# Scan decays formed from running sums that a DMA spreads over the partitions

## The chip, the cores and the metric

One core of a Trainium2 chip runs the whole program. The metric is device time in microseconds, as the median of several runs. The engines are named as in the profile: PE is TensorE (PEld its weight loads), DVE is VectorE, ACT is ScalarE, POOL is GpSimd, SP is the engine that issues most DMAs.

## What is computed

The reference is a backbone of two layers over 256 latent tokens with 256 context tokens ahead of them. Layer 0 is attention beside a convolution module, then a dense feed-forward. Layer 1 is a bidirectional state-space mixer (a chunked scan), then a feed-forward with two of eight experts for each token. The change is in the scan. For one direction the reference has, with chunks of 128 tokens:

```python
a = (dt * a_coef).reshape(b, nc, CHUNK, SSM_GROUPS, HEADS_PER_GROUP)
a_cs = jnp.cumsum(jnp.moveaxis(a, 2, -1), axis=-1)
...
lower = jnp.tril(jnp.ones((CHUNK, CHUNK), dtype=bool))
seg = jnp.exp(jnp.where(lower, a_cs[..., :, None] - a_cs[..., None, :], -jnp.inf))
cb = jnp.einsum('bclgn,bcsgn->bcgls', cc, bc)
y_diag = jnp.einsum('bcgls,bcgels,bcsgep->bclgep', cb, seg, xc)
y_off = jnp.einsum('bclgn,bcgepn,bcgel->bclgep', cc, start, jnp.exp(a_cs))
```

The second direction is the same on the flipped sequence, and both results are added, with a skip term `d_skip * x`. There are 32 heads in 4 groups of 8. `a_coef` is negative, so all running sums fall.

## The kernel before

The program is written as units (a projection of 512 output columns, say), which a `run` loop walks through; generators such as the convolution and the scan run beside them, a few steps after each unit (`later`, `tick`). A scheduler then sets the order on each engine from this program order, from priorities and from a simulated timeline. Each engine runs its own list strictly in that order.

The stage around the change is layer 1's mixer, 745 to 1055 us. TensorE projects the hidden state in units `odd_b`, `odd_c`, four `odd_x` and four `odd_z`; each weight is split into a high part (ACT, L161 or, for the output projection, L157) and a low part (DVE or POOL in turn, L164; DVE, L158), and each product is three matmuls (L243 to L245). ACT copies the sums of a projection into padded tiles (L1050); a convolution of seven taps follows, one tap on ACT (L1066) and six on DVE (L1072), then a Silu (L1126) and transposes (L1088). The output projection `odd_out` ends the stage, and the expert layer follows, whose weights stream through the buffers that the stage leaves.

The scan (`odd_ssd`) is called once for each of the four groups, as soon as its convolution is done. It forms the states at the block borders (L1178 to L1196), then works on two latent blocks of 128 tokens, and in each on two units of four heads; that makes 16 units. In a unit, with partitions as source tokens s and columns as target tokens l:

- ACT (L1215) and POOL (L1217) multiply triangular masks with the high and the low part of the decay exponents, into two pairs of tiles `tri`; four matmuls (L1232, with the strict masks GTr and LTr as weights) add them up to the segment sums of both directions in one PSUM tile `pD`; ACT takes exp (L1235) into `E`.
- DVE masks the products of C and B once per block (L1205, L1206: `cb`); POOL multiplies them with the step sizes of each direction (L1225: two tiles `cd`), DVE adds the two (L1228) and multiplies with E (L1236).
- Four matmuls (L1240) multiply E with x. Per block, two matmuls add the part of the states (L1243), POOL forms the skip term (L1245), DVE adds up (L1248 to L1252), and the gate follows (L1257, L1258).

`odd_dt_fin` forms the step sizes `dt` (one column each per head and direction: 0 to 31 forward, 32 to 63 backward) and the exponents once, ahead of the scan; TensorE forms their running sums there (L986, L987) into `pcv`, from which exp gives `ecum`. Tiles come from rings of buffers: `tri` has 4, `cd` 3, `E` 2, the PSUM tag `t` 3.

## Time and profile before

| what | value |
|---|---|
| median of 3 runs | 1942.05 us (1939.05 to 1944.78) |
| profiled execution | 1943.61 us |
| its span | 1941.8 us |
| mean granted TensorE clock | 0.962 of full |
| busy: PE, DVE, ACT, POOL | 1796.3, 728.4, 509.5, 259.1 us |
| HBM read | 486.07 MB |

The profile gives busy times of each engine, a picture of the span in 40 slices (48.5 us each), the chain of work that ended last, and groups of equal instructions. A busy share over the whole span is a mean over stages that have different limits; so the stage of the scan is read by itself, in windows. Matmuls are pipelined: one of 512 columns is shown with 390 ns, while equal ones start closer together.

### The profile page before, as it was taken

The numbers are of one execution on the slowest core, as the hardware profiler recorded it, in microseconds if no ns is written. First come the engines' busy times: TensorE is split into PE (matmuls) and PEld (weight loads), VectorE is DVE, ScalarE is ACT, GpSimd is POOL, SyncE is SP. The second block draws the span as 40 slices with busy tenths as digits, with TensorE's granted clock in tenths as the row PEclk, the third lists the DMA queues.
The fourth block names the chain that finished last, engine by engine and source line by source line (L and its number), as shares of the span: only waits on it lengthen the run. The fifth ranks groups of instructions, "written<-read, shape, count | busy, mean of one in ns | idle before, by whom it ended". The sixth has DMA issues, their size and how long they took to land.

```text
span 1941.8 us, 33657 instructions
## 1 busy us (share of the span) xinstructions
PE 1796.3 (93%) x14444; PEld 1120.8 (58%) x14444; DVE 728.4 (38%) x1118; ACT 509.5 (26%) x927; POOL 259.1 (13%) x231
## 2 busy tenths in 40 slices
PE   6999998999999989988888899999998999899964
PEld 3775356788888868766666445445534464436411
DVE  3396545334343457889987210101010101001001
ACT  3434453321222246655564200100000000001000
POOL 0064000000000024465663000000000000000000
PEclk8999989999999999999999899999999999999975
DMA  7443665323223233212145899999999999999995
GB/s 290 170 162 137 235 188 182 130 87 109 87 87 109 87 122 109 87 64 89 65 162 195 304 386 418 412 418 416 418 417 418 417 416 409 418 418 413 418 412 205
DMA packets 126538, 489.47 MB, mean 252 GB/s; under 512 B 10752, under 2 KB 17704, under 8 KB 97704
## 3 DMA queue, kind: packets, MB, share of 16 engines
q1 hardware_dynamic: 126376, 487.18, 65.2%
q8 instruction: 117, 1.92, 0.4%
q14 instruction: 45, 0.37, 0.1%
HBM read 486.07 MB, written 1.08 MB: 251 GB/s over the span
## 4 chain that ended last, share of the span: by engine, by line
PE 64%; DMA 19%; DVE 11%; ACT 3%; issue 2%; POOL 1%; SPq 0%; DVEq 0%; ACTq 0%; POOLq 0%
PE h L1515 17%; PE g L243 9%; PE g L244 9%; DMA t<-in_od_ex_w_dram 9%; PE g L245 9%; DMA raw<-in_od_ex_w_dram 8%; PE y L1580 7%; DVE cv L1072 6%; PE g L347 1%; PE h L1468 1%; PE o L775 1%; PE g L752 1%; DVE whl L164 1%; DMA raw<-in_ev_w_in_dram 1%; PE h L1604 1%
## 5 line engine op out<-in xcount | busy, mean ns | idle before, releaser
L1515 PE MATMUL h<-t,xe 128*32 128x512 f32 (+1 forms) x2576 | 252.7, 542 | 12.8 <-DMA t<-in_od_ex_w_dram 12.7
L1515 PE MATMUL h<-raw,xe 128*32 128x384 f32 (+1 forms) x2288 | 230.2, 551 | 13.6 <-DMA raw<-in_od_ex_w_dram 13.6
L244 PE MATMUL g<-t,whl 128*128 128x512 f32 (+1 forms) x608 | 238.0, 392 | 0.0
L245 PE MATMUL g<-t,whl 128*128 128x512 f32 (+1 forms) x608 | 235.9, 393 | 0.8 <-POOL whl L164 0.8
L243 PE MATMUL g<-t,whl 128*128 128x512 f32 (+1 forms) x608 | 233.9, 396 | 0.7 <-ACT t L1161 0.7
L164 DVE TENSOR_TENSOR whl<-raw,whl 128x1024 fp32r<-128x1024 f32 x109 | 138.6, 1274 | 199.2 <-ACT whl L161 198.7
L161 ACT CAST whl<-raw 128x1024 fp32r<-128x1024 f32 x129 | 134.8, 1051 | 262.7 <-PE g L245 230.4
L1515 PEld LDWEIGHTS h<-t,xe 128*32 128x32 f32 x2576 | 92.2, 110 | 164.6 <-issue 109.0
L1526 DVE TENSOR_TENSOR g<-g,h 128x512 f32<-128x512 f32 (+1 forms) x38 | 23.6, 621 | 432.7 <-issue 273.4
L428 POOL TENSOR_SCALAR rsv<-sst 128x1 f32<-128x1 f32 (+1 forms) x15 | 5.2, 346 | 1303.3 <-DVE sst L421 1303.2
L244 PE MATMUL g<-whl,t 128*128 128x512 f32 (+1 forms) x432 | 169.7, 395 | 4.9 <-DVE whl L164 3.4
L1515 PEld LDWEIGHTS h<-raw,xe 128*32 128x32 f32 x2288 | 82.4, 111 | 153.1 <-issue 95.8
L245 PE MATMUL g<-whl,t 128*128 128x512 f32 (+1 forms) x432 | 165.6, 391 | 0.0
L243 PE MATMUL g<-whl,t 128*128 128x512 f32 (+1 forms) x432 | 162.3, 395 | 2.5 <-DVE t L641 1.2
L1580 PE MATMUL y<-t,hT 128*32 128x256 f32 x2336 | 136.9, 391 | 13.1 <-DMA t<-in_od_ex_w_dram 13.1
L1523 ACT ACTIVATE g<-h 128x512 f32<-128x512 f32 (+1 forms) x38 | 20.7, 544 | 451.0 <-PE h L1515 451.0
L243 PEld LDWEIGHTS g<-t,whl 128*128 128x128 f32 x608 | 116.4, 192 | 28.7 <-issue 2.6
L245 PEld LDWEIGHTS g<-t,whl 128*128 128x128 f32 x608 | 116.0, 191 | 25.2 <-issue 1.9
L244 PEld LDWEIGHTS g<-t,whl 128*128 128x128 f32 x608 | 116.7, 192 | 23.6 <-issue 1.0
L1580 PE MATMUL y<-raw,hT 128*32 128x256 f32 x1920 | 111.1, 387 | 8.9 <-DMA raw<-in_od_ex_w_dram 8.9
L1580 PEld LDWEIGHTS y<-t,hT 128*32 128x32 f32 x2336 | 74.4, 112 | 73.8 <-DMA t<-in_od_ex_w_dram 21.1
L1594 DVE TENSOR_TENSOR ys<-y,g2r 128x512 f32<-128x512 f32 (+1 forms) x12 | 6.6, 577 | 262.5 <-PE y L1580 262.5
(348 smaller groups left out, 2232.0 us busy)
## 6 DMA issues: line engine op xcount, KB each, us to landing
t<-in_od_ex_w_dram SPq DMA_DIRECT2D x130, 1024.0 KB, 19.5
raw<-in_od_ex_w_dram SPq DMA_DIRECT2D x110, 1024.0 KB, 19.8
t<-in_od_ex_w_dram SPq DMA_DIRECT2D x68, 768.0 KB, 15.0
raw<-in_od_ex_w_dram SPq DMA_DIRECT2D x60, 768.0 KB, 14.9
raw<-in_ev_ff_w_dram SPq DMA_DIRECT2D x32, 1024.0 KB, 5.4
raw<-in_ev_ada_w_dram SPq DMA_DIRECT2D x24, 1024.0 KB, 6.9
raw<-in_od_ada_w_dram SPq DMA_DIRECT2D x24, 1024.0 KB, 5.3
raw<-in_od_w_in_dram SPq DMA_DIRECT2D x20, 1024.0 KB, 5.1
```

What stands on the lines that cost most here:

```text
L161: self.nc.scalar.copy(hv, v[:, k0:k0 + m])
L164: eng.tensor_tensor(lv, v[:, k0:k0 + m], hv.bitcast(F32), op=ALU.subtract)
L243: mm(out, l[0], r[0], start=start, stop=False)
L244: mm(out, l[0], r[1], start=False, stop=False)
L245: mm(out, l[1], r[0], start=False, stop=stop)
L347: nc.tensor.matmul(st["p"][32 * j:32 * j + 32], self.cs[:, k, 6 - 2 * i:38 - 2 * i], wv, start=k < 4, stop=k >= 4, tile_position=(0, 32 * j))
L752: nc.tensor.matmul(sc[c][:, :nk], self.qT[s, r, b * P:(b + 1) * P], self.kT[s, :nk], start=True, stop=True, tile_position=(64 * c, 0))
L1072: nc.vector.scalar_tensor_tensor(v, pads[i + j][:, 0:ns, t:t + 256], self.cvw(t, c0 + i + j), v, op0=ALU.mult, op1=ALU.add)
L1515: nc.tensor.matmul(st[i][g][32 * p:32 * p + 32, :n], st["x"][:, k, 32 * g:32 * g + 32], wv[:, n * p:n * p + n], start=k == 0, stop=k == KD ...
L1523: nc.scalar.activation(st["g"][g], st[0][g][:, :n], AF.Silu)
L1526: nc.vector.tensor_mul(st["g"][g], st["g"][g], st[1][g][:, :n])
L1580: nc.tensor.matmul(st["y"][g // 2][32 * q:32 * q + 32, g % 2 * 256:g % 2 * 256 + 256], st["hT", s][:, c, g, 32 * p:32 * p + 32], wv[:, 256 ...
```

## The change

The segment sums are no longer added up by matmuls. Running sums of both directions are kept per token and head (`cum`: columns 0 to 31 the forward sum, 32 to 63 the backward sum less the forward one), transposed, written to DRAM once, and read back so that each partition holds a row of sums over the target tokens l: two DMAs per unit on ACT's queue, `f` with the forward sums and `r` with the difference, issued up to two units ahead (`load_rows`). ACT turns `r` into relu(column - row), DVE subtracts it from `f`, and ACT takes exp with the negated column `ncf` as its bias. For l after s the relu is 0 and the forward decay is left; for l ahead of s it turns it into the backward one. The step sizes come by one affine operation on ACT per head, `LE * (dt forward - dt backward) + dt backward`. The product of C and B is read from PSUM, unmasked. On the diagonal both directions count, so the backward share of it goes into the skip factor `skip`. The four `tri` buffers now hold the rows.

Per unit there were 8 ACT products, 2 + 2 POOL products, 4 matmuls, 1 exp of 128x512, 1 DVE sum and 1 DVE product; now there are 2 DMAs, 4 relus, 4 affine operations and 4 exps of 128x128 on ACT, and 1 DVE subtraction and 2 DVE products.

```diff
@@ -922,10 +922,6 @@
                     nc.sync.dma_start(dp[:, i, 32 * j:32 * j + 32], A[f"{nme}_{d}"].partition_broadcast(P)[:, 0])
             self.dsk = self.op.tile([P, 32], F32, name="dsk")
             nc.sync.dma_start(self.dsk, A["od_d_skip"].partition_broadcast(P)[:, 0])
-            self.GTr = self.op.tile([P, P], F32R, name="GTr")
-            self.LTr = self.op.tile([P, P], F32R, name="LTr")
-            nc.scalar.copy(self.GTr, self.GT)
-            nc.scalar.copy(self.LTr, self.LT)
             st["p"] = self.ps("y")
 
         def mm(k, wh, wl):
@@ -970,12 +966,6 @@
         a = t4("da")
         nc.vector.scalar_tensor_tensor(a, dt, -1.0, ea.unsqueeze(1).to_broadcast([P, 4, 64]), op0=ALU.mult,
                                        op1=ALU.mult)
-
-        ar = self.op.tile([P, 2, 64], F32R, name="ar")
-        self.al = self.op.tile([P, 2, 64], F32, name="al")
-        nc.scalar.copy(ar, a[:, 2:4])
-        self.ah = ar.bitcast(F32)
-        nc.vector.tensor_sub(self.al, a[:, 2:4], self.ah)
         yield
         f, k = slice(0, 32), slice(32, 64)
 
@@ -998,6 +988,23 @@
         yield
         self.ecum = self.op.tile([P, 2, 64], F32, name="ecum")
         nc.scalar.activation(self.ecum, pcv, AF.Exp)
+
+
+        self.cum = self.op.tile([P, 2, 64], F32, name="cum")
+        nc.vector.tensor_copy(self.cum[:, :, f], pcv[:, :, f])
+        nc.vector.tensor_tensor(self.cum[:, :, k], pcv[:, :, k], self.cum[:, :, f], op=ALU.subtract)
+        self.ncf = self.op.tile([P, 2, 32], F32, name="ncf")
+        nc.vector.tensor_scalar(self.ncf, self.cum[:, :, f], -1.0, None, op0=ALU.mult)
+        self.ddt = self.op.tile([P, 2, 32], F32, name="ddt")
+        nc.vector.tensor_sub(self.ddt, dt[:, 2:4, f], dt[:, 2:4, k])
+        pr = self.ps()
+        for b in range(2):
+            nc.tensor.transpose(pr[:64, b * P:(b + 1) * P], self.cum[:, b], self.ident)
+        r = self.wk([P, 512], "cd", bufs=3)[:64, :256]
+        nc.scalar.copy(r, pr[:64, 0:256])
+        d = self.drp.tile([2, 64, P], F32, name=self.nm("cumd"))
+        nc.sync.dma_start(d.rearrange("b h l -> h b l"), r.rearrange("h (b l) -> h b l", b=2))
+        self.cumd = d.rearrange("b (v h) l -> b v (h l)", v=2)
         self.cdec = self.op.tile([P, 64], F32, name="cdec")
         nc.scalar.activation(self.cdec, pe, AF.Exp)
         self.wdec = t4("wdec")
@@ -1179,6 +1186,21 @@
                                                                     op=ALU.mult)
             return xw
 
+
+        units = [(b, q) for b in (2, 3) for q in range(2)]
+        rows = {}
+
+        def load_rows(i):
+            if i < len(units):
+                b, q = units[i]
+                rows[i] = [self.wk([P, 4, P], "tri", bufs=4) for _ in range(2)]
+                for v in range(2):
+                    nc.scalar.dma_start(rows[i][v].rearrange("p h l -> p (h l)"),
+                                       self.cumd[b - 2, v, 1024 * g + 512 * q:1024 * g + 512 * q + 512]
+                                       .partition_broadcast(P))
+
+        load_rows(0)
+        load_rows(1)
         start = {}
         for d in range(2):
             first, second = (2, 3) if d == 0 else (3, 2)
@@ -1201,39 +1223,35 @@
             lat = slice((b - 2) * P, (b - 1) * P)
             pcb = self.ps()
             nc.tensor.matmul(pcb[:, 0:P], self.BT[:, g, lat], self.CT[:, g, lat], start=True, stop=True)
-            cb = self.wk([P, 2, P], "cb", bufs=1)
-            nc.vector.tensor_mul(cb[:, 0], pcb[:, 0:P], self.LE)
-            nc.vector.tensor_mul(cb[:, 1], pcb[:, 0:P], self.GE)
+
+            own = self.wk([P, 2, P], "cb", bufs=1)
+            nc.vector.tensor_mul(own[:, 0], pcb[:, 0:P], self.ident)
+            nc.vector.tensor_reduce(own[:, 1, 0:1], own[:, 0], axis=AX.X, op=ALU.add)
+            skip = own[:, 1, 8:16]
+            nc.vector.scalar_tensor_tensor(skip, self.dt[:, b, 32 + 8 * g:40 + 8 * g], own[:, 1, 0:1],
+                                           self.dsk[:, 8 * g:8 * g + 8], op0=ALU.mult, op1=ALU.add)
             yd = self.ps("y")
             for q in range(2):
-                tri = []
-                for d in range(2):
-                    h0 = 32 * d + 8 * g + 4 * q
-                    m = (self.LE, self.GE)[d]
-                    th = self.wk([P, 4, P], "tri", F32R, bufs=4)
-                    for i in range(4):
-                        nc.scalar.mul(th[:, i], m, self.ah[:, b - 2, h0 + i:h0 + i + 1])
-                    tl = self.wk([P, 4, P], "tri", F32R, bufs=4)
-                    nc.gpsimd.tensor_tensor(tl, m.unsqueeze(1).to_broadcast([P, 4, P]),
-                                            self.al[:, b - 2, h0:h0 + 4].unsqueeze(2).to_broadcast([P, 4, P]),
-                                            op=ALU.mult)
-                    tri += [th, tl]
-                cd = []
-                for d in range(2):
-                    h0 = 32 * d + 8 * g + 4 * q
-                    t = self.wk([P, 4, P], "cd", bufs=3)
-                    nc.gpsimd.tensor_tensor(t, cb[:, d].unsqueeze(1).to_broadcast([P, 4, P]),
-                                            self.dt[:, b, h0:h0 + 4].unsqueeze(2).to_broadcast([P, 4, P]), op=ALU.mult)
-                    cd.append(t)
-                nc.vector.tensor_tensor(cd[0], cd[0], cd[1], op=ALU.add)
+                i = 2 * (b - 2) + q
+                f, r = rows.pop(i)
+                E = self.wk([P, 4, P], "E", bufs=2)
+                M = self.wk([P, 4, P], "cd", bufs=3)
+
+                for j in range(4):
+                    h = 8 * g + 4 * q + j
+                    nc.scalar.activation(r[:, j], r[:, j], AF.Relu, scale=-1.0, bias=self.cum[:, b - 2, 32 + h:33 + h])
+                nc.vector.tensor_tensor(f, f, r, op=ALU.subtract)
+                for j in range(4):
+                    h = 8 * g + 4 * q + j
+                    nc.scalar.activation(M[:, j], self.LE, AF.Identity, scale=self.ddt[:, b - 2, h:h + 1],
+                                         bias=self.dt[:, b, 32 + h:33 + h])
                 yield
-                pD = self.ps()
-                for i, t in enumerate(tri):
-                    nc.tensor.matmul(pD, (self.GTr, self.LTr)[i // 2], t.rearrange("p h l -> p (h l)"),
-                                     start=i == 0, stop=i == 3)
-                E = self.wk([P, 4, P], "E", bufs=2)
-                nc.scalar.activation(E, pD.rearrange("p (h l) -> p h l", h=4), AF.Exp)
-                nc.vector.tensor_mul(E, E, cd[0])
+                for j in range(4):
+                    h = 8 * g + 4 * q + j
+                    nc.scalar.activation(E[:, j], f[:, j], AF.Exp, bias=self.ncf[:, b - 2, h:h + 1])
+                load_rows(i + 2)
+                nc.vector.tensor_tensor(E, E, pcb[:, 0:P].unsqueeze(1).to_broadcast([P, 4, P]), op=ALU.mult)
+                nc.vector.tensor_mul(E, E, M)
                 yield
                 for j in range(4):
                     s = slice((4 * q + j) * 64, (4 * q + j) * 64 + 64)
@@ -1242,7 +1260,7 @@
             for d in range(2):
                 nc.tensor.matmul(po[d], self.CT[:, g, lat], start[d, b], start=True, stop=True)
             y = self.wk([P, 512], "yt", bufs=3)
-            nc.gpsimd.tensor_mul(hd(y), xb(b), self.dsk[:, 8 * g:8 * g + 8].unsqueeze(2).to_broadcast([P, 8, 64]))
+            nc.gpsimd.tensor_mul(hd(y), xb(b), skip.unsqueeze(2).to_broadcast([P, 8, 64]))
             yield
             t = [self.wk([P, 512], "yt", bufs=3) for d in range(2)]
             nc.vector.tensor_tensor(y, y, yd, op=ALU.add)
```

What this does to the order: first POOL's list in the scan, where the second latent block of the first group ends and the second group begins. Before (`tri` is the low part of the masked exponents, `cd` the step sizes times `cb`):

```order
L1225 TENSOR_TENSOR cd_6056<-cb_6038,dt 128x512
L1225 TENSOR_TENSOR cd_6058<-cb_6038,dt 128x512
L1225 TENSOR_TENSOR cd_6087<-cb_6038,dt 128x512
L1217 TENSOR_TENSOR tri_6078<-kc,al 128x512
L1225 TENSOR_TENSOR cd_6089<-cb_6038,dt 128x512
L1217 TENSOR_TENSOR tri_6085<-kc,al 128x512
L164 TENSOR_TENSOR whl_6306<-raw_6304,whl_6306 128x1024
L1217 TENSOR_TENSOR tri_6207<-kc,al 128x512
L1217 TENSOR_TENSOR tri_6214<-kc,al 128x512
```

And now (`xw` are the weighted inputs of the border states, `whl` low parts of weights):

```order
L1185 TENSOR_TENSOR xw_6156<-t_1016_5878,wdec 128x512
L1185 TENSOR_TENSOR xw_6158<-t_1016_5878,wdec 128x512
L164 TENSOR_TENSOR whl_6287<-raw_6285,whl_6287 128x1024
L1185 TENSOR_TENSOR xw_6172<-t_1016_5878,wdec 128x512
L1185 TENSOR_TENSOR xw_6174<-t_1016_5878,wdec 128x512
L164 TENSOR_TENSOR whl_6360<-raw_6358,whl_6360 128x1024
L164 TENSOR_TENSOR whl_6424<-raw_6422,whl_6424 128x1024
L164 TENSOR_TENSOR whl_6502<-raw_6500,whl_6502 128x1024
L1263 TENSOR_TENSOR yt_6276<-t_1016_5878,cb_6190 128x512
```

Between the low parts of the weights only the states' inputs and the skip term are left; the skip term now reads `cb`, the tile that holds `skip`.

ACT's list in the first group. Before (`tri` the masked exponents, one `E` per unit):

```order
L1235 ACT_TABLE_LOAD
L1235 ACTIVATE E_5866<-t_5861 128x512
L1215 ACTIVATE tri_6042<-kc,ar 128x128 x4
L1215 ACTIVATE tri_6049<-kc,ar 128x128 x4
L1089 COPY t_1013_5869<-t_5970 128x4x128
L1161 ACT_TABLE_LOAD
L1161 ACTIVATE t_895_4997<-g_5887 128x512
L1161 ACTIVATE t_896_4998<-g_5888 128x512
L1235 ACT_TABLE_LOAD
L1235 ACTIVATE E_5929<-t_5924 128x512
L1089 COPY t_1013_5869<-t_5976 128x4x128
L1215 ACTIVATE tri_6073<-kc,ar 128x128 x4
```

And now, where the first group's last two units meet the second group (`tri` numbers 6152 and 6153 are `f` and `r` of one unit, 6237 and 6238 of the next, `cumd` the sums in DRAM, the `cd` tile the step sizes):

```order
L1251 ACTIVATE E_6046<-tri_5872,ncf 128x128 x4
L1251 ACTIVATE E_6067<-tri_5929,ncf 128x128 x4
L1096 COPY t_1016_5878<-t_5979 128x4x128
L1276 ACTIVATE yt_5943,yss<-t_895_4997 128x512
L1198 DMA tri_6153<-cumd_5406 128x512
L1198 DMA tri_6237<-cumd_5406 128x512
L1246 ACTIVATE cd_6248<-kc,dt,ddt 128x128 x4
L1242 ACTIVATE tri_6153<-tri_6153,cum 128x128 x4
L1246 ACTIVATE cd_6472<-kc,dt,ddt 128x128 x4
L161 CAST whl_6206<-raw_6106 128x1024
L1198 DMA tri_6238<-cumd_5406 128x512
```

The DMA of `tri_6153` stands behind the exps whose buffer it fills again, and its relu (L1242) only four affine operations (L1246) behind it. The DMA of `tri_6238` waits for a subtraction on DVE.

DVE's list near the end of the first group. Before:

```order
L1236 TENSOR_TENSOR E_5929<-E_5929,cd_5919 128x512
L1228 TENSOR_TENSOR cd_6056<-cd_6056,cd_6058 128x512
L1248 TENSOR_TENSOR yt_5940<-yt_5940,y_5841 128x512
L1228 TENSOR_TENSOR cd_6087<-cd_6087,cd_6089 128x512
L1236 TENSOR_TENSOR E_6066<-E_6066,cd_6056 128x512
L1252 TENSOR_TENSOR yt_5940<-yt_5940,yt_5942 128x512
L164 TENSOR_TENSOR whl_6221<-raw_6122,whl_6221 128x1024
L1257 TENSOR_TENSOR t_895_4997<-t_895_4997,yt_5940 128x512
```

And now (L1243 is the subtraction, L1253 the product with the PSUM tile, L1254 the one with the step sizes):

```order
L1253 TENSOR_TENSOR E_6046<-E_6046,t_6039 128x512
L1254 TENSOR_TENSOR E_6046<-E_6046,cd_6047 128x512
L1253 TENSOR_TENSOR E_6067<-E_6067,t_6039 128x512
L1254 TENSOR_TENSOR E_6067<-E_6067,cd_6068 128x512
L1243 TENSOR_TENSOR tri_6152<-tri_6152,tri_6153 128x512
L1268 TENSOR_TENSOR yt_6140<-t_6089,ecum 128x512
L1269 TENSOR_TENSOR yt_6139<-yt_6139,yt_6140 128x512
L164 TENSOR_TENSOR whl_6206<-raw_6106,whl_6206 128x1024
L1266 TENSOR_TENSOR yt_6092<-yt_6092,y_6045 128x512
L1270 TENSOR_TENSOR yt_6092<-yt_6092,yt_6139 128x512
L1275 TENSOR_TENSOR t_896_4998<-t_896_4998,yt_6092 128x512
L1243 TENSOR_TENSOR tri_6237<-tri_6237,tri_6238 128x512
```

The subtraction of `tri_6152` and `tri_6153` stands right behind the products of the exps ahead of it, and the gate of the block, a low part of weights and the next group's states stand behind it.

## Rows read from the trace of the kernel before

**Rows 1.** Page, busy tenths in 40 slices: VectorE, then the DMA engines.

```profile
DVE  3396545334343457889987210101010101001001
...
DMA  7443665323223233212145899999999999999995
```

**Rows 2.** Windows: us; PE, PEld, DVE, ACT, POOL busy (instructions); clock, DMA share, GB/s.

```profile
780.00:1060.00 280.00, 250.02 (x1066) 187.30 (x1065) 244.83 (x259) 165.07 (x305) 156.71 (x103) 0.95 0.30 102
840.00:1055.00 215.00, 191.01 (x826) 141.49 (x824) 188.19 (x201) 132.27 (x257) 132.83 (x92) 0.96 0.28 97
1100.00:1900.00 800.00, 756.50 (x9518) 358.37 (x9510) 77.02 (x176) 44.37 (x91) 0.00 (x0) 0.98 1.01 411
```

**Rows 3.** Chain that ended last in 840 to 1055 us, shares by line.

```profile
by line: DVE cv L1072 25.4%; issue 9.3%; PE g L243 5.4%; PE g L244 5.4%; PE g L245 5.0%; DVE whl L164 4.6%; DVE whl L158 4.5%; POOL cd L1225 4.4%; DVE cd L1228 3.8%; DVE st L1195 2.8%; DVE E L1236 2.8%; PE y L1240 2.3%; ACT tri L1215 2.2%; 
```

**Rows 4.** Waits in 840 to 1055 us: waiting <- releaser: us, times, longest.

```profile
PEld g L244 <- DVE whl L164: 5.1, 3, 3.4
...
PEld t L1088 <- DVE yt L1250: 4.6, 4, 1.8
PEld y L1240 <- DVE E L1236: 4.6, 5, 1.9
```

**Rows 5.** Tiles yt, cd, tri: count, shortest/median/longest ns, first and last start.

```profile
L1250 DVE TENSOR_TENSOR yt<-t,ecum x16: 674/678/692, 851.2 to 1037.8; 128x512 f32<-128x512 f32 x16
...
L1251 DVE TENSOR_TENSOR yt<-yt,yt x8: 678/687/1524, 853.4 to 1039.2; 128x512 f32<-128x512 f32 x8
...
L1225 POOL TENSOR_TENSOR cd<-cb,dt x32: 1036/1042/2017, 846.7 to 1038.7; 128x512 f32<-128x512 f32 x32
L1228 DVE TENSOR_TENSOR cd<-cd,cd x16: 677/1510/1526, 849.8 to 1041.3; 128x512 f32<-128x512 f32 x16
...
L1217 POOL TENSOR_TENSOR tri<-kc,al x32: 1036/1484/2032, 778.2 to 1037.3; 128x512 fp32r<-128x512 f32 x32
```

**Rows 6.** Timelines of PE, DVE and SP: start us, us, instruction.

```profile
804.20 0.40 PE L243 MATMUL g<-t,whl 128*128 128x512 f32 x1
804.43 0.39 PE L244 MATMUL g<-t,whl 128*128 128x512 f32 x1
...
959.27 0.74 DVE L1072 SCALAR_TENSOR_TENSOR cv<-opad,cvb__1241,cv 128x512 f32<-128x512 f32 x1
...
812.42 0.37 SPq L148 DMA_DIRECT2D raw<-in_od_w_in_dram  x1
```

**Rows 7.** Groups by form, 780 to 1060 us: busy us, mean ns, idle before.

```profile
L1072 DVE SCALAR_TENSOR_TENSOR cv<-opad,cvb__1241,cv 128x512 f32<-128x512 f32 x48 | 57.8, 1232 | 0.0
L1072 DVE SCALAR_TENSOR_TENSOR cv<-opad,cva,cv 128x512 f32<-128x512 f32 x48 | 47.0, 1009 | 2.1 <-ACT cv L1066 1.7
...
L1228 DVE TENSOR_TENSOR cd<-cd,cd 128x512 f32<-128x512 f32 x16 | 20.1, 1258 | 8.7 <-POOL cd L1225 8.7
L1236 DVE TENSOR_TENSOR E<-E,cd 128x512 f32<-128x512 f32 x16 | 15.5, 971 | 1.0 <-ACT E L1235 0.9
...
L1217 POOL TENSOR_TENSOR tri<-kc,al 128x512 fp32r<-128x512 f32 x31 | 44.0, 1432 | 1.8 <-PE t L1232 1.8
L1225 POOL TENSOR_TENSOR cd<-cb,dt 128x512 f32<-128x512 f32 x32 | 40.5, 1284 | 23.3 <-DVE cb L1205 19.7 <-DVE cd L1228 3.6
...
L1215 ACT ACTIVATE tri<-kc,ar 128x128 fp32r<-128x128 f32 x120 | 37.1, 393 | 9.4 <-PE t L1232 9.4
...
L1235 ACT ACTIVATE E<-t 128x512 f32<-128x512 f32 x16 | 9.4, 590 | 0.1
L1235 ACT ACT_TABLE_LOAD x7 | 9.0, 1283 | 0.1
...
L1232 PE MATMUL t<-tri,GTr 128*128 128x512 f32 x32 | 12.5, 447 | 4.9 <-DVE st L1196 2.7 <-ACT tri L1215 1.9 <-POOL tri L1217 0.3
```

**Rows 8.** DMA issues: KB each, median us from issue to landing.

```profile
raw<-in_od_w_in_dram SPq DMA_DIRECT2D x20, 1024.0 KB, 5.1
...
dtpar<-in_od_dt_bias_f_dram SPq DMA_DIRECT2D x1, 16.0 KB, 2.8
```

## The prediction

> **What bounds the kernel now.** First the busy line of VectorE and that of the DMA engines over the whole span [rows 1]: VectorE is busiest from the sixteenth to the twenty-second slice (about 730 to 1070 us), and from the twenty-fourth slice on the DMA engines are full to the end. So there are two regimes. Behind 1100 us the expert weights stream at a DMA share of 1.01 [rows 2]; that tail has a fixed length, and it starts when the scan stage lets go of its tiles. What the change saves ahead of it reaches the end one to one, unless something else sets the stage's end.
>
> Then the stage itself. In 840 to 1055 us, 215 us long, VectorE is busy 188.2 us, TensorE 191.0, ScalarE 132.3 and GpSimd 132.8 us [rows 2]. The chain that ended last there goes a quarter through the convolution's VectorE line L1072, and after the projections' matmuls through the scan's own POOL L1225, DVE L1228, DVE E L1236 and ACT L1215 [rows 3]. The longest waits of TensorE's loads are for VectorE's results (L164, L1250, L1236) [rows 4]. VectorE is the engine that is late; TensorE is the next floor.
>
> Third, why VectorE is late. Its 128x512 operations come in two lengths: L1251 takes 678 ns at its shortest and 1524 at its longest, L1228 677 or, as its median, 1510; a GpSimd operation of the same shape (L1225) takes 1036 or up to 2017. L1250, one of whose operands lies in PSUM, stays within 674 to 692 [rows 5]. So VectorE and GpSimd slow each other where both read two SBUF operands; it costs VectorE 1510 - 677 = 0.83 us each time.
>
> **The change part by part**, in the profiled execution (1943.61 us around a span of 1941.8; the median of the runs is 1942.05, 1.6 us lower).
>
> *TensorE.* 64 matmuls of L1232 go, half of them the 32 with GTr that the row counts [rows 7]. Equal matmuls start 0.23 us apart [rows 6]: 64 x 0.23 = -14.7 us, inside an engine that is 89% busy. Two small transposes come, beside 826 matmuls in the stage [rows 2]; I set them at nothing.
>
> *GpSimd.* 32 operations of L1217 (31 of them in the window, 44.0 us) and 32 of L1225 (40.5 us) go, 84.5 us [rows 7] of the 156.7 that it is busy in 780 to 1060 us [rows 2]. For itself that is off the path, but it spares VectorE collisions. Four groups carry most of what VectorE loses, against 0.74 us for an undisturbed L1072 [rows 6] and 0.68 for the others [rows 5]: L1072 (1.232 - 0.74) x 48 = 23.6 and (1.009 - 0.74) x 48 = 12.9, L1228 (1.258 - 0.68) x 16 = 9.2, L1236 (0.971 - 0.68) x 16 = 4.7 [rows 7], together 50.4 us. By GpSimd's share, 84.5/156.7 = 54%, the removed operations cause **27 us** of it. The ends: 0, if the GpSimd operations left over (weights, L1245) collide as often in their place, and 64 x 0.83 = 53 us, if each removed operation cost one collision. I take 27, which comes from the means of many.
>
> The Trainium skill ("SBUF — State Buffer", section "SBUF: two separate sides") says that the two engines take turns at a shared pair of ports, and that whoever comes second is blocked for the other's whole instruction. By it a removed operation could free up to its own undisturbed 1.04 us, 64 x 1.04 = 66 us, an estimate, in place of 27 or 53; the rows show no VectorE operation of this shape stretched by more than about 0.85.
>
> *VectorE.* The sum of L1228 becomes the subtraction f - r of the same shape, nothing gained; the product L1236 stays, now with the step sizes; a second product, with pcb, comes: 16 x 0.68 = +10.9 us, one operand in PSUM like L1250. Per latent block two masks become one product of their shape, a reduce and a tiny operation, which I take as even. VectorE comes to 188.2 - 27 + 11 = 172 us, with ends of 146 and 199.
>
> *ScalarE.* Per unit, 8 operations of 0.393 us and one of 0.590 become 12 of 0.393: 16 x (4.72 - 3.73) = +15.8 us. The order has 23 table loads for 27 of 1.28 us each: -5.1 us [rows 7]. It now issues 32 DMAs. The trace has none on ScalarE; the nearest row is SP's, 0.37 us [rows 6], so 0 to 11.8 us, and I take 11.8. ScalarE comes to 132.3 + 22.5 = 155 us of 215. It has room, as long as it isn't made to wait.
>
> *The new wait* is just that. The relus of a unit wait for a row load that ScalarE issued itself, and behind a waiting relu stand the casts of the projections' weights, the copies of their sums and the Silu of the convolution, for which TensorE and VectorE wait. At the place shown, four affine operations, 1.6 us, lie between load and relu. No row shows a 256 KB load spread over all partitions; the nearest are a spread 16 KB with 2.8 us and 1024 KB with 5.1 us [rows 8]. I take 3.3, as far between them as the size is. Elsewhere up to eight operations lie between, and the load is mostly covered. A wait of 1.7 us at a third of the 16 units costs ScalarE 9 us of its 60 us of room. VectorE meets the wait at the subtraction: 3.3 + 1.6 for the relus, less about 2 us of products ahead of it, 3 us at two places of the order. Of these 6 us I charge 4 to the end.
>
> The Trainium skill ("DMA: Bandwidth & Descriptors", section "Anatomy of one DMA — SWDGE (gpsimd) path") gives 2 us plus the bytes over 436 GB/s, an estimate of 2.6 us for 256 KB, fitted on another issuing path. By it the stalls would be 0.7 us shorter each and the sum about 1 us better. No row here has this load.
>
> Once, at the start, SP writes the running sums to DRAM and the first row loads wait for it. The cover is the convolution work that has to come before the scan: its first L1225 starts at 846.7 us, while the first L1217, which reads the step sizes times the coefficients just as the running sums do, starts at 778.2 [rows 5]. Without that cover it would be two landings, 6 us. PSUM's t slots are held longer, as pcb lives on to the second product; in exchange pD is gone. I set both at nothing.
>
> **Sum.** TensorE -14.7. Of its 14.3 us of waiting for VectorE [rows 4] a third goes, -5, since VectorE falls by 16 of 188 us. New stalls +4. Together -16 us: 1943.6 - 16 = 1927.6 in the profiled execution, 1926 as a median.
>
> **The rivals.**
>
> *Every collision comes back* (chance 0.15). VectorE falls to 146 us and nothing of TensorE's waits for it stays: -14.7 - 14.3 = -29 us, 1913, or a little below where TensorE's smaller waits go too. For it: L1228's median is its long form [rows 5]. Against: L1225's median is its short one, so at least half of them were not slowed. The page on the SBUF would have it so, with a turn for each whole instruction.
>
> *The gain is eaten in the stage* (0.20). The subtraction stalls by 3 us at five or more of 16 places, 15 us, and takes back what TensorE saves: 1936 to 1942. For it: ScalarE works strictly in order, and VectorE now hangs on it once more. Against: the loads are issued up to two units ahead.
>
> *ScalarE becomes the bound* (0.13). If a row load lands late, each of 16 units costs ScalarE the landing less 1.6 us of cover. From 155 us it has 60 to give, 3.75 a unit, so this decides from a landing of 5.4 us. At 6 us it is 155 + 16 x 4.4 = 225 us, 10 more than the stage has now: 1952, slower. For it: 1024 KB of weights, which share the DMA engines, take 5.1 us themselves [rows 8]. Against: the DMA share in the stage is 0.28 [rows 2].
>
> **How the numbers follow.** The forecast has 0.52, between 1918 and 1936. A measurement of this kernel tells about 0.3%, 6 us, from no change. Faster than 1936: the forecast, the first rival and a part of the second, 0.74; slower than 1948: most of the third, 0.11; the rest is 0.15. The range for eight in ten goes down past the first rival, to 1910, and up to 1942, the end of the second.
>
> **What would show it.** Right: GpSimd busy about half as long in the stage, the means of L1072's two groups lower by about a quarter of a microsecond, no L1232, the expert stage some 16 us earlier, and the tail as long as before. The waits at the relus and the subtraction should be a few us in all. Wrong: if L1072 keeps its means (the GpSimd work left over collides instead), if ScalarE's waits for row loads sum to tens of us, or if the tail grows by what the stage saves.

## The result, and the profile after

The changed kernel takes 1921.82 us (median of four runs, 1918.18 to 1924.88) against 1943.07 us of the kernel before, measured beside it (1939.05 to 1944.78). The ratio is 0.9889, with a 95% interval of 0.9873 to 0.9904: 21 us faster, where the forecast was 1926 us and 17 us less than before. The profiled execution took 1918.18 us around a span of 1916.4.

The busy line of VectorE and that of the DMA engines, from the page of the changed kernel, answer [rows 1]:

```profile
DVE  3395546334334367789886110102010101001001
...
DMA  8543765323223233423357899999999999999995
```

From the 16th slice to the 24th VectorE has 778988611 for 788998721, so it falls off sooner, and the DMA engines have 342335789 for 321214589: the row loads, and the expert weights that come earlier. To be exact, I measure the stage from one mark to another: from ScalarE's copy of the step sizes (L936 before, L932 after, at 744.92 and 740.38 us) to the first matmul of the expert stage (1078.74 and 1053.81). It is **333.8 us before and 313.4 after, 20.4 us less**. What follows it takes 863.1 and 862.6 us; the tail keeps its length, as forecast. The 4.5 us by which the stage begins earlier are not the change's: over the fourteen profiles below that mark lies between 738.6 and 746.0 us.

One row of windows for exactly that stage, the kernel before (length; busy PE, PEld, DVE, ACT, POOL with instructions; granted clock, DMA share, GB/s):

```profile
744.92:1078.74 333.82, 295.89 (x1361) 226.69 (x1359) 288.19 (x345) 198.27 (x364) 175.75 (x113) 0.96 0.34 119
```

and the changed kernel:

```profile
740.38:1053.81 313.43, 282.25 (x1299) 215.90 (x1297) 264.31 (x372) 208.22 (x408) 92.88 (x49) 0.94 0.45 155
```

Read by TensorE, busy time fell by 13.6 us (forecast 14.7) and idle time from 37.9 to 31.2 us, by 6.7 (forecast 1: 5 less of waiting, 4 of new stalls). GpSimd lost 82.9 us (84.5), ScalarE gained 9.9 (10.7, its DMA issues not counted as busy), VectorE lost 23.9 (16). The total agrees, its parts less so. The longest waits of TensorE's matmuls for VectorE and for ScalarE in the stage, before (waiting <- releaser: us, times, longest):

```profile
PE t L1191 <- DVE xw L1178: 7.2, 2, 5.3
PE g L244 <- DVE whl L164: 3.4, 3, 2.7
...
PE t L1232 <- ACT tri L1215: 1.9, 3, 1.1
```

and after:

```profile
PE g L243 <- ACT opad L1057: 3.5, 2, 2.7
PE t L1213 <- ACT cv L1133: 3.3, 1, 3.3
...
PE g L244 <- DVE whl L164: 2.9, 1, 2.9
```

Summed over all such rows, TensorE waits 26.6 us for VectorE before and 9.9 after, 16.7 less; for ScalarE 6.5 and 15.0, 8.5 more; for GpSimd 1.1 and 2.7.

VectorE's groups and ScalarE's, in 770 to 1045 us of the changed kernel (busy us, mean ns, idle before), answer [rows 7]; L1079 is the convolution, L1072 before:

```profile
L1079 DVE SCALAR_TENSOR_TENSOR cv<-opad,cva,cv 128x512 f32<-128x512 f32 x48 | 50.9, 1081 | 6.1 <-ACT cv L1073 5.9
L1079 DVE SCALAR_TENSOR_TENSOR cv<-opad,cvb__1241,cv 128x512 f32<-128x512 f32 x48 | 43.9, 935 | 0.0
...
L1243 DVE TENSOR_TENSOR tri<-tri,tri 128x512 f32<-128x512 f32 x16 | 12.8, 798 | 9.0 <-ACT tri L1242 9.0
...
L1254 DVE TENSOR_TENSOR E<-E,cd 128x512 f32<-128x512 f32 x16 | 10.7, 681 | 0.1
L1253 DVE TENSOR_TENSOR E<-E,t 128x512 f32<-128x512 f32 x16 | 10.5, 678 | 0.1
...
L1246 ACT ACTIVATE cd<-kc,dt,ddt 128x128 f32<-128x128 f32 x64 | 26.1, 485 | 12.6 <-DVE E L1254 11.1 <-issue 1.5
...
L1242 ACT ACTIVATE tri<-tri,cum 128x128 f32<-128x128 f32 x64 | 20.5, 395 | 7.6 <-DMA tri<-cumd 7.6
```

The convolution's two groups together fell from 104.8 to 94.8 us; the operation in the place of the old sum (L1243 for L1228) from 20.1 to 12.8; the last product (L1254 for L1236) from 15.5 to 10.7. The gain of the convolution lies in one of its groups, by 0.30 us an operation; the other is 0.07 longer than before. The four groups together lose 22.1 us where 27 were forecast, and 10.5 us (forecast 10.9) come back as the product L1253. The waits that the change adds show too: 7.6 us at the relus for row loads, 9.0 us at the subtraction. The row loads among the changed kernel's DMA issues (KB, median us to landing):

```profile
tri<-cumd ACTq DMA_DIRECT2D x32, 256.0 KB, 3.7
```

### The profile page after: what moved, and what is told of

Read it like the earlier page. It is cut to its first block, busy times and chain, and to the rows that moved or that the text cites. A ratio compares the mean times of both kernels' runs of the same rounds, so it can differ in the third digit from the quotient of the medians.

```text
span 1916.4 us, 33607 instructions
## 1 busy us (share of the span) xinstructions
PE 1778.7 (93%) x14382; PEld 1105.9 (58%) x14382; DVE 704.2 (37%) x1145; ACT 519.0 (27%) x969; POOL 176.6 (9%) x167
## 5 line engine op out<-in xcount | busy, mean ns | idle before, releaser
L1533 PE MATMUL h<-t,xe 128*32 128x512 f32 (+1 forms) x2576 | 252.7, 542 | 12.8 <-DMA t<-in_od_ex_w_dram 12.8
L244 PE MATMUL g<-t,whl 128*128 128x512 f32 (+1 forms) x608 | 235.2, 387 | 0.0
L245 PE MATMUL g<-t,whl 128*128 128x512 f32 (+1 forms) x608 | 231.6, 387 | 0.9 <-POOL whl L164 0.8
L243 PE MATMUL g<-t,whl 128*128 128x512 f32 (+1 forms) x608 | 231.4, 392 | 0.8 <-ACT opad L1057 0.8
L164 DVE TENSOR_TENSOR whl<-raw,whl 128x1024 fp32r<-128x1024 f32 x109 | 137.7, 1266 | 204.0 <-ACT whl L161 203.6
L1598 PE MATMUL y<-t,hT 128*32 128x256 f32 x2336 | 136.5, 390 | 13.5 <-DMA t<-in_od_ex_w_dram 13.5
L243 PEld LDWEIGHTS g<-t,whl 128*128 128x128 f32 x608 | 115.1, 190 | 28.5 <-ACT t L133 1.9
L245 PEld LDWEIGHTS g<-t,whl 128*128 128x128 f32 x608 | 114.6, 189 | 24.4 <-DVE whl L164 1.1
L244 PEld LDWEIGHTS g<-t,whl 128*128 128x128 f32 x608 | 114.9, 189 | 23.0 <-issue 0.7
L1598 PEld LDWEIGHTS y<-t,hT 128*32 128x32 f32 x2336 | 74.4, 112 | 74.1 <-DMA t<-in_od_ex_w_dram 21.3
```

The source lines that it names most:

```text
L164: eng.tensor_tensor(lv, v[:, k0:k0 + m], hv.bitcast(F32), op=ALU.subtract)
L243: mm(out, l[0], r[0], start=start, stop=False)
L244: mm(out, l[0], r[1], start=False, stop=False)
L245: mm(out, l[1], r[0], start=False, stop=stop)
L1533: nc.tensor.matmul(st[i][g][32 * p:32 * p + 32, :n], st["x"][:, k, 32 * g:32 * g + 32], wv[:, n * p:n * p + n], start=k == 0, stop=k == KD ...
L1598: nc.tensor.matmul(st["y"][g // 2][32 * q:32 * q + 32, g % 2 * 256:g % 2 * 256 + 256], st["hT", s][:, c, g, 32 * p:32 * p + 32], wv[:, 256 ...
```

## The experiments

The question is which part of the work, taken away, made TensorE's stage shorter: its own 64 matmuls, or the GpSimd operations that lengthened VectorE's. Twelve kernels answer it. All times stand against runs of the kernel before on the same chip (medians of 1942.7 to 1944.2 us). The table gives, of each profile, the row for the stage as above; idle is the stage's length less TensorE's busy time. One such reading may be off by the few us by which the runs of a kernel differ. The edits are given in short, and `...` stands for what is left out. The scheduler sets the order anew for each kernel, so an edit can also move instructions that it doesn't name; e3, e4 and n3 stay nearest to the changed kernel's order, m1 and m2 depart far from that of the kernel before.

| kernel | median us, ratio to before (95%) | stage us | PE busy / idle | clock | DVE | ACT | POOL |
|---|---|---|---|---|---|---|---|
| before | – | 333.8 | 295.9 / 37.9 | 0.96 | 288.2 | 198.3 | 175.8 |
| after | 1921.8, 0.9889 (0.9873–0.9904) | 313.4 | 282.3 / 31.2 | 0.94 | 264.3 | 208.2 | 92.9 |
| e1 affine part only | 1949.4, 1.0024 (1.0010–1.0037) | 340.5 | 301.5 / 39.0 | 0.93 | 268.1 | 222.6 | 131.1 |
| e2 rows part only | 1926.9, 0.9909 (0.9892–0.9926) | 318.4 | 281.6 / 36.8 | 0.94 | 280.1 | 185.3 | 136.7 |
| e3 after + 64 matmuls | 1925.8, 0.9906 (0.9891–0.9921) | 316.9 | 290.2 / 26.7 | 0.96 | 261.5 | 206.1 | 88.6 |
| e4 after + 64 GpSimd products | 1953.6, 1.0044 (1.0031–1.0057) | 347.4 | 287.2 / 60.2 | 0.90 | 308.9 | 206.1 | 173.4 |
| m1 before − 64 matmuls | stage only | 333.0 | 282.4 / 50.6 | 0.94 | 282.8 | 192.9 | 180.6 |
| m2 before − 64 GpSimd products | stage only | 306.4 | 286.0 / 20.4 | 0.97 | 252.7 | 203.5 | 89.0 |
| e6 after − one product on VectorE | stage only | 300.8 | 274.3 / 26.4 | 0.97 | 256.8 | 210.5 | 88.9 |
| e7 after − affine operations | stage only | 305.5 | 273.0 / 32.5 | 0.97 | 263.2 | 182.4 | 92.5 |
| n1 after, nothing on GpSimd | 1909.2, 0.9816 (0.9799–0.9834) | 297.1 | 273.4 / 23.7 | 0.96 | 254.8 | 212.7 | 4.2 |
| n2 after, low parts on VectorE | 1906.3, 0.9807 (0.9793–0.9820) | 296.3 | 272.3 / 24.0 | 0.96 | 251.0 | 215.3 | 43.2 |
| n3 after, rows from SyncE | 1921.9, 0.9879 (0.9861–0.9897) | 314.2 | 281.9 / 32.3 | 0.94 | 263.1 | 208.7 | 93.7 |
| b1 before, low parts on VectorE | 1925.0, 0.9904 (0.9886–0.9921) | 318.0 | 289.8 / 28.2 | 0.96 | 276.7 | 202.7 | 128.5 |

**Each half of the change alone.** e1 keeps the segment sums of the kernel before and takes the new step sizes:

```diff
-                cd = [GpSimd: cb[:, d] x dt, d = 0, 1]; cd[0] += cd[1]
+                M[:, j] = Identity(LE, scale=ddt, bias=dt)        # ScalarE, 4 times
...
-                nc.vector.tensor_mul(E, E, cd[0])
+                nc.vector.tensor_tensor(E, E, pcb (broadcast), op=ALU.mult)
+                nc.vector.tensor_mul(E, E, M)
```

> The kernel before with the second half of the change alone: the step sizes come from ScalarE's affine operation, the diagonal and the skip factor from own, and E is multiplied twice on VectorE; the segment-sum matmuls, their split operands on GpSimd and ScalarE, and the exp from PSUM stay. It drops 32 of GpSimd's products (40.5 us of its time) and no matmul. Theory (TensorE's 14.7 us plus some VectorE relief): no TensorE work goes, about half of the collisions go, 1932 to 1940 us, middle 1936. Rival 1, only the matmuls count: 1943 us. Rival 2, only VectorE's relief from GpSimd counts: half of the 21 us, 1932 us. Rival 3, ScalarE is close to the bound: with 26 us more on it and nothing taken off, slower than 1943 us, up to 1955 us.

It is 0.24% slower, inside the span of its rival 3. Yet VectorE is 20.1 us less busy in the stage than before. The longest waits of TensorE in e1's stage, and the longest of VectorE, say where the relief went:

```profile
PE t L1234 <- ACT tri L1220: 6.8, 6, 3.3
PE t L1246 <- DVE yt L1253: 5.6, 1, 5.6
...
DVE E L1238 <- ACT E L1237: 23.6, 9, 4.9
```

L1234 is the segment-sum matmul, L1220 its operand from ScalarE; in the kernel before this pair waits 1.9 us. L1237 is the exp, for which VectorE waits 0.9 us before [rows 7]. In all VectorE waits 55.6 us for ScalarE in e1's stage and 20.6 before: what it saved it stood, since ScalarE, 24.3 us busier, was late. In the program the affine operations stand ahead of the unit's exp. e2 takes the other half, decays from the spread rows, and keeps masks, GpSimd products and their sum:

```diff
-                tri operands, four matmuls into pD, E = exp(pD)
+                r[:, j] = Relu(cum - r[:, j]);  f -= r;  E[:, j] = Exp(f[:, j] - cum_f)
```

> The kernel before with the first half of the change alone: decays from the running sums spread by DMA, relu and subtraction, no segment-sum matmuls, no split operands; the step sizes stay as masks on VectorE, 32 products on GpSimd and their sum on VectorE. It drops 64 matmuls (14.7 us of TensorE) and 32 GpSimd operations (44 us). Theory: the matmuls' 14.7 us and half of the collisions, 1924 to 1930 us, middle 1927. Rival 1, only the matmuls count: 1922 us, as with the whole change. Rival 2, only the relief counts: 1932 us.

1926.9 us, the middle that the theory gave. TensorE is 14.3 us less busy there and idles 1.1 less, so this run alone would speak for the matmuls' length. The halves don't add up, +5 and -17 for -21 together: the affine operations cost most where ScalarE still has the operands to make as well.

**The two suspects put back.** e3 issues 64 matmuls that nobody reads in the changed kernel, e4 64 GpSimd products (and, not shown, it keeps `own` in a smaller tile):

```diff
+                for n in range(4):                                # e3
+                    nc.tensor.matmul(pD, GTr, GTr (broadcast), start=n == 0, stop=n == 3)
...
+                for n in range(4):                                # e4
+                    nc.gpsimd.tensor_tensor(z, LE or GE (broadcast), dt (broadcast), op=ALU.mult)
```

> The changed kernel with 64 matmuls of 512 columns put back, four in each of the 16 units at the place of the old segment-sum matmuls; they read a constant, wait for no operand and nothing reads their result. Theory: TensorE's time comes back whole, 64 x 0.23 = 14.7 us, 1934 to 1938 us. Rival 1, only the matmuls count, waits for their operands included: 14.7 us or a little more, up to 1943 us. Rival 2, TensorE isn't the bound and only VectorE's relief counts: 1922 us.

> The changed kernel with 64 products of 128x512 put back on GpSimd, four in each of the 16 units; they read a constant and a step size and nothing reads their result (it is written as bf16 into one buffer). GpSimd's busy time goes back up by some 80 us. Theory: VectorE slows by 25 to 30 us in the stage, and a fourth to a third of it reaches the end, 1927 to 1933 us. Rival 1, only the matmuls count: 1922 us. Rival 2, only the relief counts: 1940 us or more.

Both weights of the prediction, the whole of TensorE's time and a third of VectorE's, fall here. The matmuls cost about 4 us (1921.8 to 1925.8; the intervals of the ratios overlap, and at their far ends it would be 9), not 14.7: TensorE is 7.9 us busier and idles 4.5 us less. The GpSimd products, which no engine waits for, cost **32 us**, ten more than the whole change brought. VectorE is 44.6 us busier for them with the same 372 instructions, and the idle time of TensorE nearly doubles. The convolution's two groups take 119.3 us there in place of 94.8:

```profile
L1079 DVE SCALAR_TENSOR_TENSOR cv<-opad,cva,cv 128x512 f32<-128x512 f32 x48 | 66.7, 1420 | 4.9 <-ACT cv L1073 4.8
L1079 DVE SCALAR_TENSOR_TENSOR cv<-opad,cvb__1241,cv 128x512 f32<-128x512 f32 x48 | 52.6, 1119 | 0.0
```

TensorE's longest waits in e4's stage are all for VectorE:

```profile
PE t L1213 <- DVE xw L1185: 13.9, 2, 10.1
PE g L245 <- DVE whl L164: 10.6, 1, 10.6
PE g L244 <- DVE whl L164: 7.0, 1, 7.0
```

TensorE's own waits for GpSimd sum to 4.4 us there, 2.7 without the products, and VectorE's to 1.1 us with and without them. So it is not GpSimd's longer queue that VectorE waits for: its own operations take longer.

**The two suspects taken away from the kernel before.** m1 drops the 64 matmuls and lets exp read their first operand, m2 drops the 64 GpSimd products and keeps every matmul:

```diff
-                pD = the four matmuls; E = exp(pD)                # m1
+                E = exp(tri[0])
...
-                    tl = GpSimd: m x al;  cd = GpSimd: cb x dt    # m2
+                    tri += [th, th];  cd[0] = cb[:, 0] + cb[:, 1] on VectorE
```

Leaving such terms out changes which experts the tokens are sent to, and so the work behind the stage (whole times above 3000 us). These two, e6 and e7 are read in the stage alone, and their forecasts as differences.

> The kernel before without its 64 segment-sum matmuls: exp reads the first split operand in SBUF instead of the PSUM sum, so the decays are wrong; the operands are still made on ScalarE and GpSimd. Theory now (VectorE's chain with GpSimd's collisions sets the stage, TensorE has room for these matmuls): a gain of 2 to 6 us against the kernel before, 1938 to 1942 us. Rival of the prediction (TensorE's work counts whole): 14.7 us, 1929 us. Rival 3 (what the matmuls cost is not their length but TensorE standing in order until their operands are there): 10 us or more, 1934 us or less.

> The kernel before without the 64 GpSimd products that the change takes away: the high parts are multiplied twice instead of the low ones, and VectorE adds the two masks and not the two weighted ones, so the decays' last digits and the step sizes are wrong; matmuls, ScalarE and VectorE have as many instructions as before. Theory now (VectorE with GpSimd's collisions sets the stage): 20 to 30 us faster than the kernel before, 1914 to 1924 us. Rival of the prediction (a third of the relief of 27 us reaches the end): 9 us, 1935 us. Rival 3 (TensorE's waits for operands): 5 us or less, 1939 us or more.

The row of the stage in m1:

```profile
742.05:1075.03 332.98, 282.36 (x1296) 215.01 (x1295) 282.76 (x345) 192.88 (x360) 180.64 (x113) 0.94 0.34 120
```

and in m2:

```profile
740.98:1047.36 306.38, 285.97 (x1360) 223.32 (x1359) 252.73 (x345) 203.51 (x368) 88.95 (x49) 0.97 0.37 128
```

In m1 TensorE is 13.5 us less busy and idles 12.7 more, and the stage is 0.8 us shorter. But the added waiting is not for VectorE (26.7 us for 26.6 before): it is for ScalarE, 15.0 us for 6.5, and for GpSimd, 5.6 for 1.1. One single wait is most of it, from the timelines of ScalarE and TensorE:

```profile
790.52 2.45 ACT L1215 ACTIVATE tri<-kc,ar 128x128 fp32r<-128x128 f32 x8
792.86 2.02 ACT L1050 COPY opad<-g 128x512 f32<-128x512 f32 x4
...
793.49 0.79 PE L243 MATMUL g<-t,whl 128*128 128x512 f32 x1 [8.35 <-ACT opad L1050]
```

The exp of m1 waits for no matmul any more, and the scheduler put masks and exps of the scan in front of this copy, on which the projection hangs; in the kernel before TensorE does not wait there. **So m1 is no clean removal of the matmuls.** Without that wait its gain would be some 9 us, an estimate (0.8 + 8.35). So it leaves open what the matmuls are worth between about 1 and 9 us, and e3 remains the cleaner test.

m2 has all matmuls, and its stage is 27.4 us shorter, TensorE's idle time nearly halved. Its order differs as well, and VectorE waits 8.7 us less for GpSimd's products; but e4 agrees with it from the other side. So the GpSimd products alone are worth more than the change. m2's stage is also 7 us shorter than the changed kernel's, with the matmuls still in it: about so much the change seems to have given back with what it adds.

**What the changed kernel's own new work costs.** e6 leaves out VectorE's product L1253, e7 the affine operations (VectorE multiplies by the mask in their stead):

```diff
-                nc.vector.tensor_tensor(E, E, pcb (broadcast), op=ALU.mult)     # e6
...
-                M[:, j] = Identity(LE, scale=ddt, bias=dt)                      # e7
-                nc.vector.tensor_mul(E, E, M)
+                nc.vector.tensor_mul(E, E, LE (broadcast))
```

> The changed kernel without the product of E with the diagonal block on VectorE, 16 x 0.68 = 10.9 us less on VectorE, nothing else taken away (its output lacks that factor). Theory now: VectorE sets the stage, 7 to 11 us faster, 1911 to 1915 us. Rival of the prediction (a third of VectorE's time reaches the end): 4 us, 1918 us. Rival 4 (ScalarE's queue sets the stage): within 2 us of 1922 us.

> The changed kernel without the 64 affine operations of ScalarE, 26 us less on ScalarE; VectorE multiplies by the mask alone, in as many instructions (the step sizes are missing from the output). Theory now: ScalarE is not on the path, 0 to 4 us faster, 1918 to 1922 us. Rival 4 (ScalarE's queue sets the stage): 10 us or more, 1912 us or less.

e6's stage is 12.7 us shorter, and that is a floor: its first expert matmul waits for its weights.

```profile
1043.29 1.14 PE L1485 MATMUL h<-pm,h 128*128 128x96 f32 x4 [1.74 <-DMA t<-in_od_ex_w_dram]
```

The row is from e6's timeline of TensorE. VectorE is 7.5 us less busy there, for 10.9 us of products taken out. Counted to the last step of the scan it is even 24.8 us; why more than was taken out, stays open. Without the product the PSUM tile of the diagonal block is also free earlier, and the order differs; no run separates these from VectorE's time. e7 brought 7.9 us for 25.8 us off ScalarE, between the two forecasts: ScalarE counts for about a third. TensorE's waits for it in the stage fall from 15.0 to 9.1 us, but its idle time does not (32.5 for 31.2): it waits more for VectorE, and the same matmuls are busy 9.2 us less, at a granted clock of 0.97 for 0.94.

**The step that follows.** If GpSimd costs VectorE that much, the rest of its work in the stage should go too, even onto VectorE. n2 moves the weights' low parts (L164), n1 the states' inputs and the skip product as well:

```diff
-    LO_MIX = (1, 0)
+    LO_MIX = (1,)            # n2, n1, b1: every low part on VectorE
...
-    XW = 2
+    XW = 0                   # n1 alone, with the skip product on nc.vector
```

n3 leaves GpSimd alone and moves the row loads to another queue:

```diff
-                    nc.scalar.dma_start(rows[i][v] ...
+                    nc.sync.dma_start(rows[i][v] ...
```

> The changed kernel with all that GpSimd still does in the stage moved to VectorE: the low parts of the weights, the states' inputs and the skip product, 73.5 us off GpSimd, and on VectorE 14 x 1.21 + 16 x 0.68 + 8 x 0.68 = 33 us more at its undisturbed lengths. Theory now (what counts is VectorE's time, and GpSimd's work lengthens it by some 50 us here): VectorE ends with 15 to 20 us less, 1902 to 1912 us. Rival (VectorE's own work counts, GpSimd's collisions count little): 25 to 35 us slower, 1947 to 1957 us.

> The changed kernel with only the weights' low parts moved from GpSimd to VectorE: 39.7 us off GpSimd, 17 us more on VectorE at its undisturbed length, against 39.7/73.5 of 50 us of collisions, 27 us. Theory now: 10 us less on VectorE, 1910 to 1917 us. Rival (the collisions count little): 10 to 17 us slower, 1932 to 1939 us.

> The changed kernel with the row loads issued from SyncE's queue instead of ScalarE's: ScalarE loses 32 issues of 0.33 us and the 9.0 us that it stood at one waiting for the subtraction; SyncE's weight loads stand behind that wait instead. Theory now (ScalarE's time counts a third, as 26 us less of it brought 8 us): 3 to 6 us faster, 1916 to 1919 us. Rival (the weight loads come late behind the waiting row loads): slower by 3 us or more, 1925 us or more.

n2 is the fastest kernel here, **1906.3 us, 1.9% under before**. VectorE has 17 operations more and is 13.3 us less busy. Its groups in 770 to 1045 us, to be read against the two convolution rows of the changed kernel above:

```profile
L1079 DVE SCALAR_TENSOR_TENSOR cv<-opad,cva,cv 128x512 f32<-128x512 f32 x48 | 38.0, 814 | 2.1 <-ACT cv L1073 2.0
L164 DVE TENSOR_TENSOR whl<-raw,whl 128x1024 fp32r<-128x1024 f32 x29 | 36.8, 1268 | 4.3 <-ACT whl L161 4.3
L1079 DVE SCALAR_TENSOR_TENSOR cv<-opad,cvb__1241,cv 128x512 f32<-128x512 f32 x48 | 36.4, 780 | 0.1
```

The same 96 convolution operations take 74.4 us in place of 94.8. n1 gains no more (1909.2): a further 39 us off GpSimd are paid with 24 operations on VectorE, 3.9 us more in all. n3 changes nothing to be measured: neither the 9.0 us that ScalarE stood at two issues of row loads nor SyncE's standing in its place shows at the end. That both are off the path, or that they cancel, the run doesn't tell apart.

Last, the same one line in the kernel before:

> The kernel before with one edit, the weights' low parts moved from GpSimd to VectorE, all else as before: some 48 us off GpSimd (16 or 17 x 3.0), 16 x 1.21 = 19 us more on VectorE at its undisturbed length. Theory now (GpSimd's collisions lengthen VectorE by 82 us here, half a us for each us of GpSimd): 25 us of collisions less, 5 us less on VectorE in all, and as VectorE's time reaches the end nearly whole, 1934 to 1941 us. Rival (large operands collide most, as in the changed kernel where this edit gave 15 us): 1925 to 1931 us. Rival (with GpSimd's 85 us of products still there, VectorE's own work counts): 1946 to 1958 us.

```profile
738.59:1056.56 317.97, 289.82 (x1361) 226.46 (x1359) 276.67 (x362) 202.65 (x367) 128.53 (x96) 0.96 0.36 127
```

1925.0 us, the first rival's size and not the 5 us of the theory: one line does nearly what the whole change did. The theory's price of half a us of VectorE for each us of GpSimd was too low for the low parts. From the rows of the stage, with a low part at 1.22 us on VectorE (the mean of n1's 29) and an input or skip at 0.68:

| edit | GpSimd us | VectorE us, beside the work moved to it | VectorE per GpSimd |
|---|---|---|---|
| e4 against after (64 products) | +80.6 | +44.6 | 0.55 |
| m2 against before (64 products) | -86.8 | -35.5 | 0.41 |
| b1 against before (17 low parts) | -47.2 | -11.5 - 17 x 1.22 = -32.2 | 0.68 |
| n2 against after (17 low parts) | -49.7 | -13.3 - 17 x 1.22 = -34.0 | 0.68 |
| n1 against n2 (24 inputs and skips) | -39.0 | +3.9 - 24 x 0.68 = -12.5 | 0.32 |

The low parts hit the convolution hardest. From its 104.8 us in the kernel before 18.9 go with the 17 low parts (b1), and only 7.3 with the 64 products (m2); the first two rows are b1's, the others m2's:

```profile
L1072 DVE SCALAR_TENSOR_TENSOR cv<-opad,cvb__1241,cv 128x512 f32<-128x512 f32 x48 | 45.4, 966 | 0.0
L1072 DVE SCALAR_TENSOR_TENSOR cv<-opad,cva,cv 128x512 f32<-128x512 f32 x48 | 40.5, 870 | 3.4 <-ACT cv L1066 3.0
...
L1072 DVE SCALAR_TENSOR_TENSOR cv<-opad,cva,cv 128x512 f32<-128x512 f32 x48 | 49.0, 1049 | 4.9 <-ACT cv L1066 4.6
L1072 DVE SCALAR_TENSOR_TENSOR cv<-opad,cvb__1241,cv 128x512 f32<-128x512 f32 x48 | 48.5, 1039 | 0.0
```

b1 and n2 also have their low parts sooner, 1.37 instead of 2.72 us each and 1.27 instead of 2.83; how much of their gain is that, and not collisions, no run separates. TensorE's waits for GpSimd sum to 2.7 us in the changed kernel's stage, which speaks for the collisions.

## Why the time was right and the reasons were not

**TensorE's 14.7 us: the step that failed.** The length of the matmuls was right, and their disappearance from TensorE's busy time too. Wrong was that time taken off an engine that is 89% busy reaches the end whole. Put back alone the matmuls cost 4 us (e3); taken away alone they gave 0.8, or some 9 without the one wait that m1's order brought. In e3 TensorE idles 4.5 us less and its granted clock is higher (0.96 for 0.94): idle time and clock seem to have taken in most of the added work.

**VectorE's relief at a third: the other step that failed.** The prediction itself named VectorE as the engine that is late, and then let 5 us of TensorE's waiting for it go, a third of the 14.3 us in the three rows that it showed. Over the stage that waiting was 26.6 us, and 16.7 of it went. m2 and e4 show the price of VectorE's time: 27.4 us of the stage for 35.5 of VectorE, 33.9 for 44.6, so 0.77 and 0.76, more than twice the third. (With the 8.7 us that VectorE waits less in m2, its price is 0.62.)

**The new stalls, +4 us.** TensorE waits 8.5 us more for ScalarE and 1.6 more for GpSimd. So read in TensorE's rows, -14.7, -5 and +4 became -13.6, -16.7 and +10.

**The total was luck in part.** The first step was too large by some 11 us (e3's 4 for 14.7), the second too small by some 13 (0.77 x 23.9 = 18 where 5 stood). The total of the stage could not show it, since a balance of one profile tells where time stood, not what would free it. The prices found here, 0.77 for VectorE, a third for ScalarE and up to 4 us for the matmuls, give 15 to 19 us for the change and 10 to 14 for e2; their stages are 20.4 and 15.4 us shorter. For e1 they give 8 us of gain where its stage is 6.7 longer: where another engine comes to be late, as ScalarE there, the prices no longer hold.

**Collisions, -27 us.** The right size, with another make-up: for the four groups it is -22.1, of which the convolution has 10.0 where 54% of its loss would have been 19.7, and the scan's two operations 12.1 for 7.5. The sign that was to show it, both means of the convolution lower by a quarter of a microsecond, came in one group only. The prediction shared the collisions out by GpSimd's busy time, but for each us of it the weights' low parts, which stay, cost VectorE more than the products (0.68 and 0.41). m2, which takes only the products away, has -35.5 over all of VectorE. From the changed kernel's timelines, GpSimd with a low part

```profile
883.80 3.24 POOL L164 TENSOR_TENSOR whl<-raw,whl 128x1024 fp32r<-128x1024 f32 x1 [2.94 <-ACT whl L161]
```

and VectorE beside it and behind it:

```profile
884.71 4.20 DVE L1079 SCALAR_TENSOR_TENSOR cv<-opad,cva,cv 128x512 f32<-128x512 f32 x3
888.83 0.74 DVE L1079 SCALAR_TENSOR_TENSOR cv<-opad,cvb__1241,cv 128x512 f32<-128x512 f32 x1
```

Three convolution operations take 4.20 us, where three undisturbed ones in a row take 2.07, from n2's timeline:

```profile
889.99 2.07 DVE L1079 SCALAR_TENSOR_TENSOR cv<-opad,cvb__1241,cv 128x512 f32<-128x512 f32 x3
```

2.1 us are lost while the two engines overlap for 2.3 (884.71 to 887.04). The rule of the Trainium skill ("SBUF — State Buffer", section "SBUF: two separate sides"), a turn for the whole of the other's instruction, agrees with this place. As a price for every us of GpSimd it is too high: the table above has 0.32 to 0.68. Part of GpSimd's time meets no VectorE operation, or only one with an operand in PSUM; how much, no run counts.

**The new product, +10.9 us.** 10.5 in the trace, with its operand in PSUM undisturbed at 678 ns. In e6 the stage is 12.7 us shorter without it, though other things change there too; the prediction let it count a third with the rest.

**ScalarE.** The four affine operations take 485 ns, not the 393 of the masks' row, 6 us more in all; the issue of a row load takes 0.33 us, not 0.37. The sum was right within a us, the weight again missing: in e7 a third of it reaches the end.

**The row loads.** 3.7 us to the landing where 3.3 was taken, 7.6 us of waits at the relus for 9, 9.0 at the subtraction for 6. The two together are more than the few us that the prediction named as its sign. The estimate after the Trainium skill's page "DMA: Bandwidth & Descriptors" (section "Anatomy of one DMA — SWDGE (gpsimd) path"), 2.6 us, was too short. ScalarE's stand at a load's issue was not foreseen, and n3 gives no sign that it cost anything.

**The rivals.** A landing of 5.4 us, from which ScalarE would have become the bound, was reached by the longest (6.0) and not by the median. The subtraction did stall at five places, for 9.0 us in all and not 15, so the gain was not eaten. "Every collision comes back" was nearest for TensorE's waits (14.3 us for the 16.7 that went), with twice the collisions that came back (53 for 22.1 in the four groups) and the wrong price for the matmuls beside it.

## What to carry to other kernels

Before a busy engine's work is counted as gain, ask for whom it waits in that stage: 64 more matmuls on a TensorE that idled 31 us cost 4 us of their 14.7 (e3). In this stage GpSimd work on two SBUF operands was paid by VectorE with a third to two thirds of its length, even if nobody waited for its result; look for the largest such operands first, since moving 17 low parts to VectorE brought nearly as much as rewriting the decays (19 and 21 us). A sum that agrees with the result is no proof of its terms: put one suspect back alone, take one away alone, and look at the order before you call it alone (m1).
